# Hybrid attention, retention and MoE layer: attention shares, a stage for retention with three sets of buffers, its decay kept in its units, and no GpSimd in it

## The chip, the cores and the metric

One core of a Trainium2 chip runs the program. The metric is the device time of one execution in microseconds (us), the median over runs. Engine names in the profile: PE is TensorE's matmuls and PEld its weight loads, DVE is VectorE, ACT is ScalarE, POOL is GpSimd, SP is SyncE, which here issues most DMAs.

## The reference

One encoder layer on 2048 tokens of width 1024. A normed input is projected into seven parts, two head groups run beside each other, and a mixture of experts follows.

```python
# attention, 4 heads of 2 maps of 64, values of 128; chunk of 64, causal by chunk
s = einsum(q, k) * scale - slope * |q_pos - k_pos|        # per map
a = softmax(s[0]) - lam * softmax(s[1])
o = rmsnorm(a @ v, subln_g) * (1 - lambda_init)           # lambda_init 0.2
# retention, 4 heads, q and k of 64, v and g of 128, gamma per head
intra = (q @ k.T * 0.125) * decay[t - s >= 0] @ v
cross = (q * gamma**(t + 1)) @ state
state = state * gamma**C + (k * 0.125 * gamma**(C - 1 - s)).T @ v
o = silu(g) * head_rmsnorm(intra + cross)
# then
h = x + concat(att, ret) @ w_out
out = rmsnorm(h + moe(rmsnorm(h)))     # 4 groups top-1, 8 experts each, top-2, SwiGLU
```

## The kernel before

Large products are split in a high and a low part and done as three matmuls (L62, L63, L64 of the helper `mm3`); the result in PSUM is taken out by an ACT copy and a DVE difference (`split_psum`, L54 and L55).

**Projection** (`Proj.run`): 96 units of eight triple matmuls of 512 columns, tile `pa`. Results go to DRAM: QS, KS, VS for the attention, RT (q and k of the retention, transposed), VR and GR (its values and gate).

**Attention** (`att_head`), in three stages of 512-token row groups, (0,1), (2), (3), four heads each. For 128 query rows: scores `pS` (L350, L351) for up to 2048 keys, bias and maximum in one DVE operation (L352), exponent on ACT (L359), the difference of the two maps (reciprocal L362, `c` L363, the long product L366), transposes `pT` (L382), their split (L54, L55), value products `pO`, and in `finish` the norm (a Newton inverse root, L31 to L40, then U times r, L426, and times subg, L427, both on GpSimd).

**Retention** (`retention`), 16 blocks of 128 tokens, two at a time. `prepare` loads one pair ahead: kt, qz (with zeros in the other half), vr, gr; GpSimd forms vd = vr times decay (L481) and qd = qz times decay (L486); the gate is a tanh (L490) and a product (L491). `inner` makes a head pair's q·k (L499), transposes kt (L500), masks with rdec (L502) and copies (L504). Then per head pair: qd·state (L523), A·v (L524), kd·vd (L528), the state's step on DVE (L530). After two blocks come an inverse root (L546, L31 to L40, L548), O times r (L549) and times th (L550) on GpSimd, 1024 elements a partition each, and the store of both blocks. Two sets of the buffers exist (`bufs=2`).

**Out-projection** (`OutProj`): w_out is loaded in eight tiles (L709), split on ACT (L712) and, half of them each, GpSimd and DVE (L713), into woh and wol; the router's weights are cast by DVE (L1129). Then come 16 blocks with 48 matmuls each into `pF`, and the routing. The MoE stage is last.

Order: `merge` emits two streams in turn, by weights: attention beside the projection up to a share FA of all attention, beside retention FR, and the rest beside the out-projection. Pieces of attention are emitted at a higher priority (PRI). A scheduler then fixes each engine's order. SP's loads and stores are one queue in program order.

Of the kernel before, what the change touches and what calls it, by code (L numbers as in the profile page):

```python
# [84 lines left out]
class Proj:  # L85
# [108 lines left out]
    def colT(self, u, c, ct, g):  # L194
# [8 lines left out]
        if c == 3:  # L203
            st = self.stg.tile([128, 512], F32, name="st", tag="st")
            nc.scalar.activation(st, ps, AF.Copy)
            nc.sync.dma_start(k.RT[ct][:, ts], st)
            return
# [9 lines left out]
    def rows(self, u, c, b):  # L217
# [78 lines left out]
def att_head(k, s, h):  # L296
# [119 lines left out]
    def finish(b0, b1):  # L416
# [9 lines left out]
        nc.gpsimd.tensor_mul(u, u, r[:, :, None].to_broadcast([128, n, 128]))  # L426
        nc.gpsimd.tensor_mul(u, u, k.subg[:, None, :].to_broadcast([128, n, 128]))  # L427
# [25 lines left out]
def retention(k):  # L453
    nc, tc = k.nc, k.tc
    V, G = nc.vector, nc.gpsimd
    state, qz = [], {}
    for pr in range(2):
# [3 lines left out]
        for n in range(2):  # L461
# [3 lines left out]
            qz[pr, n] = z  # L465
    def prepare(n):
# [39 lines left out]
    nxt = prepare(0)  # L506
# [3 lines left out]
    for b in range(NB):  # L510
        if b % 2 == 0:
            X = nxt
            nxt = prepare(b // 2 + 1) if b + 2 < NB else None
            vr, O, ss = X.vr, X.O, X.ss
        bb = b % 2
        st2 = []
        for pr in range(2):
            A, kd = st[pr]
            po = k.pF.tile([128, 512], F32, name="pF")
            for s in range(2):  # L520
                ps = po[:, s * 128:(s + 1) * 128]
# [96 lines left out]
def att_consts(k, n):  # L618
# [15 lines left out]
    k.subg = k.bc.tile([128, 128], F32, name="subg")  # L634
    nc.sync.dma_start(k.subg, bcast_rows(k.da_subln_g, 128))
    nc.vector.tensor_scalar(k.subg, k.subg, 0.8, None, op0=OP.mult)


def ret_consts(k):
    nc = k.nc  # L640
    k.rdec = k.br.tile([128, 2, 256], F32, name="rdec", bufs=1)
    k.qdec = k.br.tile([128, 2, 128], F32, name="qdec", bufs=1)
    k.vdec = k.br.tile([128, 4], F32, name="vdec", bufs=1)
    k.sdec = k.br.tile([128, 2], F32, name="sdec", bufs=1)
    rel = k.br.tile([128, 128], F32, name="rel", bufs=1)
# [3 lines left out]
    nc.gpsimd.iota(rel, pattern=[[1, 128]], base=0, channel_multiplier=-1, allow_small_or_imprecise_dtypes=True)
    nc.gpsimd.iota(pos, pattern=[[1, 128]], base=1, channel_multiplier=0, allow_small_or_imprecise_dtypes=True)  # L650
    nc.gpsimd.iota(col, pattern=[[1, 1]], base=127, channel_multiplier=-1, allow_small_or_imprecise_dtypes=True)
    nc.vector.tensor_scalar(msk, rel, 0.0, 0.125, op0=OP.is_ge, op1=OP.mult)
    nc.vector.tensor_scalar(rel, rel, 0.0, None, op0=OP.max)
    for hd in range(4):
        pr, s = hd // 2, hd % 2
        rd = k.rdec[:, pr, s * 128:(s + 1) * 128]
        nc.scalar.activation(rd, rel, AF.Exp, scale=LGAM[hd])
        nc.vector.tensor_mul(rd, rd, msk)
        nc.scalar.activation(k.qdec[s * 64:(s + 1) * 64, pr, :], pos[s * 64:(s + 1) * 64], AF.Exp, scale=LGAM[hd])
        nc.scalar.activation(k.vdec[:, hd:hd + 1], col, AF.Exp, scale=LGAM[hd])  # L660
# [1269 lines left out]
```

## Time and profile before

| | |
|---|---|
| median of 3 runs | 2078.36 us (2072.5 to 2091.58) |
| profiled execution | 2069.81 us |
| its span | 2068.0 us |
| busy PE, DVE, ACT, POOL | 1939.0, 1551.5, 1122.5, 663.0 us |
| granted clock of PE, mean | 0.973 |

The span is counted from the first instruction to the last; the profiled execution's own time is 1.8 us more. Busy time is an average over stages with different limits, so the tables below are by stretch. In the profile, L12 is line 12 of the kernel; what stands behind "<-" in a list of waits is what ended the wait. A matmul's duration in the timeline includes a part that overlaps the next; the distance of two starts is the pace.

### The profile page before, as it was taken

What the parts mean: (1) busy time and instruction counts of PE and PEld (TensorE: products, weight loads), DVE (VectorE), ACT (ScalarE), POOL (GpSimd) and SP (SyncE); (2) the same over time, 40 slices, a digit from 0 to 9 for tenths busy, and PEclk for the clock granted to TensorE, in tenths of its full rate; (3) what the DMA queues carried; (4) which work ended last, traced back from release to release, by engine and by line L of the source; (5) the groups of instructions that cost most, each with busy time, mean ns of one, the idle gap of its engine ahead of it and who ended that gap; (6) DMA issues with size and microseconds to landing.
All of it is one profiled execution on the core that took longest, in us unless ns stands there. A gap on an engine that the chain in (4) does not pass through costs nothing. (4 is left out here: it accounts for less than half of the span.)

```text
span 2068.0 us, 30117 instructions
## 1 busy us (share of the span) xinstructions
PE 1939.0 (94%) x9811; PEld 1539.9 (74%) x9811; DVE 1551.5 (75%) x3462; ACT 1122.5 (54%) x1915; POOL 663.0 (32%) x362
## 2 busy tenths in 40 slices
PE   6999999999999987789999997899999999999994
PEld 5788888788888875578887775677777677777673
DVE  7355446855565578987877767989997899998874
ACT  4244445534444454555454315667776777776763
POOL 0000000010000037421101105777766468755333
PEclk9999999999999999889999997999999999999997
DMA  6655344573675457364453455899999999998993
GB/s 202 199 153 168 117 134 142 183 238 127 204 215 168 138 152 222 128 198 143 148 180 124 139 224 193 288 331 300 318 324 308 325 352 353 349 339 299 332 323 109
DMA packets 241810, 459.61 MB, mean 222 GB/s; under 512 B 27376, under 2 KB 130160, under 8 KB 240624
## 3 DMA queue, kind: packets, MB, share of 16 engines
q1 hardware_dynamic: 224384, 401.53, 57.1%
q0 software_dynamic: 16976, 55.06, 9.9%
q8 instruction: 78, 1.28, 0.2%
q10 hardware_dynamic: 288, 1.05, 0.1%
q14 instruction: 84, 0.69, 0.1%
HBM read 365.81 MB, written 91.75 MB: 221 GB/s over the span
## 5 line engine op out<-in xcount | busy, mean ns | idle before, releaser
L1485 DVE TENSOR_TENSOR ml<-mr,mh 128x1024 fp32r<-128x1024 f32 x376 | 445.6, 1211 | 32.0 <-ACT mh L1484 31.9
L1484 ACT ACTIVATE mh<-mr 128x1024 fp32r<-128x1024 f32 x376 | 385.0, 1054 | 119.1 <-PE acc L74 67.5
L1515 POOL DMA_INDIRECT xg<-XN,TA x120 | 270.0, 2250 | 70.3 <-issue 29.3
L352 DVE CUSTOM_DVE_ANT_0 p<-pS,dist 128x512 f32<-128x512 f32 (+1 forms) x320 | 187.9, 605 | 124.1 <-PE pS L351 116.3
L426 POOL TENSOR_TENSOR U<-U,r 128x512 f32<-128x512 f32 (+2 forms) x13 | 16.5, 1270 | 721.6 <-DVE r L40 619.6
L359 ACT ACTIVATE p<-p,nm 128x128 f32<-128x128 f32 (+15 forms) x128 | 153.9, 1202 | 111.8 <-DVE nm L358 111.6
L64 PE MATMUL acc<-mh,xlo 128*128 128x512 f32 x512 | 204.4, 400 | 1.6 <-DVE xlo L1557 1.6
L63 PE MATMUL acc<-ml,xhi 128*128 128x512 f32 x512 | 204.4, 399 | 0.0
L62 PE MATMUL acc<-mh,xhi 128*128 128x512 f32 x512 | 203.4, 400 | 0.1
L54 ACT ACTIVATE ah<-pT 128x512 fp32r<-128x512 f32 (+2 forms) x176 | 85.4, 498 | 138.8 <-PE pT L382 96.7
L62 PE MATMUL pa<-whi,xh 128*128 128x512 f32 x384 | 151.4, 396 | 3.2 <-ACT whi L161 2.5
L62 PE MATMUL pa<-xh,whi 128*128 128x512 f32 x384 | 152.7, 398 | 1.4 <-DVE st L58 1.4
L63 PE MATMUL pa<-wlo,xh 128*128 128x512 f32 x384 | 152.2, 397 | 1.8 <-DVE wlo L162 1.5
L64 PE MATMUL pa<-whi,xl 128*128 128x512 f32 x384 | 153.0, 399 | 0.0
L63 PE MATMUL pa<-xl,whi 128*128 128x512 f32 x384 | 152.0, 396 | 0.0
L64 PE MATMUL pa<-xh,wlo 128*128 128x512 f32 x384 | 151.6, 395 | 0.0
L162 DVE TENSOR_TENSOR wlo<-wr,whi 128x1024 fp32r<-128x1024 f32 x72 | 90.6, 1260 | 64.3 <-ACT whi L161 62.8
L350 PE MATMUL pS<-kst,qs 128*128 128x512 f32 (+1 forms) x320 | 123.3, 398 | 15.6 <-DVE cm L352 7.3
L55 DVE TENSOR_TENSOR al<-pT,ah 128x512 fp32r<-128x512 f32 (+2 forms) x176 | 97.5, 564 | 44.0 <-ACT ah L54 43.6
L62 PEld LDWEIGHTS acc<-mh,xhi 128*128 128x128 f32 x512 | 97.2, 190 | 32.5 <-ACT y L1646 0.5
L161 ACT ACTIVATE whi<-wr 128x1024 fp32r<-128x1024 f32 x72 | 76.1, 1058 | 78.6 <-PE pa L63 35.9
L64 PEld LDWEIGHTS acc<-mh,xlo 128*128 128x128 f32 x512 | 96.7, 189 | 24.3 <-DVE xlo L1557 2.1
(536 smaller groups left out, 4890.1 us busy)
## 6 DMA issues: line engine op xcount, KB each, us to landing
mr<-in_expert_w_gate_dram SPq DMA_DIRECT2D x128, 512.0 KB, 6.4
mr<-in_expert_w_up_dram SPq DMA_DIRECT2D x128, 512.0 KB, 6.5
mr<-in_expert_w_down_dram SPq DMA_DIRECT2D x128, 512.0 KB, 7.0
wr<-in_w_in_dram SPq DMA_DIRECT2D x72, 512.0 KB, 4.7
vst<-VS SPq DMA_DIRECT2D x72, 256.0 KB, 4.8
qs<-QS SPq DMA_DIRECT2D x128, 128.0 KB, 4.0
st<-in_x_dram SPq DMA_DIRECT2D x16, 512.0 KB, 4.2
VS<-st SPq DMA_DIRECT2D x32, 256.0 KB, 2.9
```

What stands on the lines that cost most here:

```text
L54: nc.scalar.activation(hi, ps, AF.Copy)
L55: return nc.vector.tensor_sub(lo, ps, hi.bitcast(F32))
L62: nc.tensor.matmul(out, s_hi, m_hi, start=start, stop=False)
L63: nc.tensor.matmul(out, s_hi, m_lo, start=False, stop=False)
L64: nc.tensor.matmul(out, s_lo, m_hi, start=False, stop=stop)
L162: nc.vector.tensor_sub(lo, r, hi.bitcast(F32))
L350: nc.tensor.matmul(x, qs[0][:, m, 0, o:o + 128], ks[m][:, a0:a1], start=True, stop=False)
L352: nc.vector.tensor_tensor_reduce(p[:, a0:a1], x, tab[:, c0 + a0:c0 + a1], SLOPES[h], -3.0e38, OP.add, OP.max, accum_out=cm[:, n:n + 1])
L359: nc.scalar.activation(p[:, :nk], p[:, :nk], AF.Exp, bias=nm, accum_out=s0 if m == 0 else s1)
L1484: self.hi_at = nc.scalar.activation(hi, r, AF.Copy)
L1485: self.lo_at = nc.vector.tensor_sub(lo, r, hi.bitcast(F32))
L1515: nc.gpsimd.indirect_dma_start(out=xg[:, g * 256:(g + 1) * 256], out_offset=None, in_=v, in_offset=bass.IndirectOffsetOnAxis(ap=ix[:, g], ...
```

## The change

The key decay is multiplied into k where the projection takes k out of PSUM (DVE, where ACT copied), and silu of the gate is formed there as well. q's decay and the matching inverse drop out: the mask rdec holds a constant per head (gamma^-128, below the diagonal), and the norm's epsilon is scaled per row (edec), since the head norm divides a row's scale out. In `retention`, vd, qd, the tanh and the gate product go, and O's two products become eight DVE operations, one a block and head. Buffers exist in three sets, and `prepare` runs two pairs ahead. In `finish`, U times r runs on DVE, and subg is multiplied into the first four tiles of w_out where they are split; all eight differences run on DVE. Attention gets a share of 0.82 beside the projection; retention is emitted as a stage by itself, after 8 units of attention.

```diff
--- before.py
+++ after.py
@@ Proj.colT
         if c == 3:
             st = self.stg.tile([128, 512], F32, name="st", tag="st")
-            nc.scalar.activation(st, ps, AF.Copy)
+            if ct < 2:
+                nc.scalar.activation(st, ps, AF.Copy)
+            else:
+                nc.vector.tensor_mul(st.rearrange("p (b t) -> p b t", t=128), ps.rearrange("p (b t) -> p b t", t=128),
+                                     k.kdec[:, ct - 2, None, :].to_broadcast([128, 4, 128]))
@@ Proj.rows
-            nc.scalar.activation(st, ps, AF.Copy)
+            if c == 4:
+                nc.scalar.activation(st, ps, AF.Copy)
+            else:
+                nc.scalar.activation(st, ps, AF.Tanh, scale=0.5)
+                nc.vector.scalar_tensor_tensor(st, st, 1.0, ps, op0=OP.add, op1=OP.mult)
@@ att_head, finish
-        nc.gpsimd.tensor_mul(u, u, r[:, :, None].to_broadcast([128, n, 128]))
-        nc.gpsimd.tensor_mul(u, u, k.subg[:, None, :].to_broadcast([128, n, 128]))
+        nc.vector.tensor_mul(u, u, r[:, :, None].to_broadcast([128, n, 128]))
@@ retention
-        for n in range(2):
+        for n in range(3):
             z = k.br.tile([128, 2, 256], F32, name=f"qz{pr}{n}", bufs=1)
...
-        X.q = [qz[pr, n % 2] for pr in range(2)]
+        X.q = [qz[pr, n % 3] for pr in range(2)]
...
-        gr = k.br.tile([128, 2, 512], F32, name="gr")
+        X.th = k.br.tile([128, 2, 512], F32, name="th")
         nc.sync.dma_start(X.vr, k.VR[ts, :].rearrange("(b p) n -> p b n", p=128))
-        nc.sync.dma_start(gr, k.GR[ts, :].rearrange("(b p) n -> p b n", p=128))
-        X.vd = k.br.tile([128, 2, 4, 128], F32, name="vd")
-        G.tensor_mul(X.vd, X.vr.rearrange("p b (h e) -> p b h e", h=4),
-                     k.vdec[:, None, :, None].to_broadcast([128, 2, 4, 128]))
-        X.qd = []
-        for pr in range(2):
-            qd = k.br.tile([128, 2, 2, 128], F32, name=f"qd{pr}")
-            G.tensor_mul(qd, X.q[pr].rearrange("p s (b t) -> p s b t", b=2),
-                         k.qdec[:, pr, None, None, :].to_broadcast([128, 2, 2, 128]))
-            X.qd.append(qd)
-        X.th = k.br.tile([128, 2, 512], F32, name="th")
-        nc.scalar.activation(X.th, gr, AF.Tanh, scale=0.5)
-        V.scalar_tensor_tensor(X.th, X.th, 1.0, gr, op0=OP.add, op1=OP.mult)
+        nc.sync.dma_start(X.th, k.GR[ts, :].rearrange("(b p) n -> p b n", p=128))
...
-    nxt = prepare(0)
+    coming = [prepare(0), prepare(1)]
+    nxt = coming.pop(0)
...
-            nxt = prepare(b // 2 + 1) if b + 2 < NB else None
+            if b + 4 < NB:
+                coming.append(prepare(b // 2 + 2))
+            nxt = coming.pop(0) if coming else None
...
-                    nc.tensor.matmul(ps, X.qd[pr][:, s, bb], state[pr], start=True, stop=False)
+                    nc.tensor.matmul(ps, X.q[pr][:, s, bb * 128:(bb + 1) * 128], state[pr], start=True, stop=False)
...
-            V.tensor_scalar(v, ss.rearrange("p a b -> p (a b)"), 1.0 / 128, EPS, op0=OP.mult, op1=OP.add)
-            rsqrt_newton(nc, rf, v, t_)
-            V.tensor_scalar(rf, rf, 0.5, None, op0=OP.mult)
-            G.tensor_mul(O, O, r[:, :, :, None].to_broadcast([128, 2, 4, 128]))
-            G.tensor_mul(O, O, X.th.rearrange("p a (h e) -> p a h e", h=4))
+            V.scalar_tensor_tensor(v, ss, 1.0 / 128, k.edec[:, None, :].to_broadcast([128, 2, 4]), op0=OP.mult, op1=OP.add)
+            rsqrt_newton(nc, r, v, t_)
+            V.tensor_scalar(r, r, 0.5, None, op0=OP.mult)
+            th = X.th.rearrange("p a (h e) -> p a h e", h=4)
+            for i in range(2):
+                for h in range(4):
+                    V.scalar_tensor_tensor(O[:, i, h], O[:, i, h], r[:, i, h:h + 1], th[:, i, h], op0=OP.mult, op1=OP.mult)
@@ key_decay (new, called ahead of the projection's loop), ret_consts
+def key_decay(k, pool):
...
+        nc.gpsimd.iota(k.kdec[:, pr], pattern=[[-1, 128]], base=127, channel_multiplier=0, allow_small_or_imprecise_dtypes=True)
...
+        nc.scalar.activation(x, x, AF.Exp, scale=LGAM[hd])
+    nc.vector.tensor_scalar(k.kdec, k.kdec, 0.125, None, op0=OP.mult)
...
+        nc.vector.tensor_scalar(k.rdec[:, pr, s * 128:(s + 1) * 128], msk, 0.0, math.exp(-128 * LGAM[hd]), op0=OP.is_ge, op1=OP.mult)
+        nc.scalar.activation(k.edec[:, hd:hd + 1], col, AF.Exp, scale=-2 * LGAM[hd])
...
+    nc.vector.tensor_scalar(k.edec, k.edec, EPS, None, op0=OP.mult)
@@ OutProj.load
-        nc.scalar.activation(hi, r, AF.Copy)
-        (nc.gpsimd if t % 2 < WOP else nc.vector).tensor_sub(lo, r, hi.bitcast(F32))
+        if t < 4:
+            nc.scalar.activation(hi, r, AF.Copy, scale=k.subg)
+            nc.vector.scalar_tensor_tensor(lo, r, k.subg, hi.bitcast(F32), op0=OP.mult, op1=OP.subtract)
+        else:
+            nc.scalar.activation(hi, r, AF.Copy)
+            nc.vector.tensor_sub(lo, r, hi.bitcast(F32))
@@ mixers
-        k.br = ctx.enter_context(tc.tile_pool(name="br", bufs=2, side="right", reuse_waits="tile"))
+        k.br = ctx.enter_context(tc.tile_pool(name="br", bufs=3, side="right", reuse_waits="tile"))
...
-        merge(tc, retention(k), 58, a, na * FR)
+        r = retention(k)
+        next(r)
+        y = 0
+        while y < FR:
+            y += next(a)
+        for _ in r:
+            pass
...
-        merge(tc, op.blocks(at), OB, a, na * (1 - FA - FR))
+        merge(tc, op.blocks(at), OB, a, na * (1 - FA) - FR)
...
-FA = 0.7
-FR = 0.12
+FA = 0.82
+FR = 8.0
```

**PE, end of the projection and start of retention** (pS scores, pO value products and pT transposes of the attention, pa the projection, pF the retention, which begins with L499, L500 of the change). Before:

```order
L63 MATMUL pO<-al,vst 128x256
L64 MATMUL pO<-ah,vst 128x256
L62 MATMUL pO<-ah,vst 128x128
L350 MATMUL pS<-kst,qs 128x512
L351 MATMUL pS<-kst,qs 128x512
L499 MATMUL pF<-qz_8149,kt 128x256
```

and of the change:

```order
L64 MATMUL pa<-whi,xl_4237 128x512
L360 MATMUL pS<-kst,qs 128x512
L361 MATMUL pS<-kst,qs 128x512
L419 MATMUL pT<-ident,oT 128x128 x2
L392 MATMUL pT<-ident,p_6111 128x128 x2
L392 MATMUL pT<-ident,p_6319 128x128 x2
```

About one step of attention moves ahead of the retention's start; in the whole projection it is 5.1 thousand columns of pS, 4.2 of pO and 0.4 of pT more.

**DVE, the last pair of retention's blocks** (r and v the inverse root of the norm, O and th retention's output and gate; p, c, S the attention's). Before:

```order
L40 SCALAR_TENSOR_TENSOR r_9647<-t_9648,r_9647 128x8
L548 TENSOR_SCALAR r_9647<-r_9647 128x8
L362 RECIPROCAL c<-s_7589 128x1
L363 SCALAR_TENSOR_TENSOR c<-c,S_7050,nlam 128x1
L366 SCALAR_TENSOR_TENSOR p_7590<-p_7636,c,p_7590 128x2048
L352 ISA p_7970,cm<-pS,dist 128x512
```

and of the change:

```order
L40 SCALAR_TENSOR_TENSOR r_9747<-t_9748,r_9747 128x8
L551 TENSOR_SCALAR r_9747<-r_9747 128x8
L372 RECIPROCAL c<-s_7210 128x1
L555 SCALAR_TENSOR_TENSOR O<-O,r_9747,th 128x128 x2
L373 SCALAR_TENSOR_TENSOR c<-c,S_6932,nlam 128x1
L555 SCALAR_TENSOR_TENSOR O<-O,r_9747,th 128x128 x6
L376 SCALAR_TENSOR_TENSOR p_7211<-p_7232,c,p_7211 128x2048
L362 ISA p_7544,cm<-pS,dist 128x512
```

The eight products on O stand on DVE between the attention's reciprocal and its long product.

**POOL, in the middle of retention.** Before, a piece of it:

```order
L486 TENSOR_TENSOR qd_9150<-qz_8157,qdec 128x512
L550 TENSOR_TENSOR O<-O,th 128x1024
L481 TENSOR_TENSOR vd<-vr,vdec 128x1024
L486 TENSOR_TENSOR qd_9354<-qz_8152,qdec 128x512
L549 TENSOR_TENSOR O<-O,r_9118 128x1024
L486 TENSOR_TENSOR qd_9356<-qz_8160,qdec 128x512
```

and all that the change leaves on POOL from retention's constants (dist, msk, col) to the first operation of the routing (xc):

```order
L626 IOTA dist 128x1536
L660 IOTA msk 128x128
L661 IOTA col 128x1
L626 IOTA dist 128x2048
L867 TENSOR_TENSOR xc<-xT 128x512 x24
```

No product of retention or of the attention's end is left there.

## Rows read from the trace of the kernel before

**Rows 1.** Stretches: us, busy PE, PEld, DVE, ACT, POOL (instructions), PEclk, DMA share, GB/s

```profile
0.00:733.00 733.00, 711.83 (x3587) 596.26 (x3588) 421.70 (x1192) 328.51 (x654) 30.12 (x58) 1.00 0.55 169
769.50:779.50 10.00, 8.75 (x66) 6.88 (x65) 8.57 (x30) 6.10 (x31) 4.07 (x3) 1.00 0.88 270
779.50:799.30 19.80, 12.46 (x66) 9.60 (x65) 11.62 (x29) 6.15 (x30) 17.34 (x10) 0.74 0.91 279
801.00:845.00 44.00, 37.73 (x242) 28.65 (x241) 43.58 (x124) 26.17 (x90) 26.02 (x13) 1.00 0.46 146
907.00:1240.00 333.00, 323.83 (x2025) 268.57 (x2025) 253.66 (x866) 139.13 (x263) 41.24 (x34) 1.00 0.48 163
```

**Rows 2.** Tile pF: duration ns min/median/max, first and last start, forms

```profile
L62 PE MATMUL pF<-woh,mh x256: 387/393/500, 907.1 to 1239.9; 128*128 128x512 f32 x128
...
L524 PE MATMUL pF<-vr,A x128: 270/275/582, 745.6 to 861.7; 128*128 128x128 f32 x128
...
L499 PE MATMUL pF<-qz,kt x64: 377/379/634, 739.1 to 858.2; 128*128 128x256 f32 x64
```

**Rows 3.** DVE by line and form, 801 to 845: count, busy us, mean ns, idle before

```profile
L352 DVE CUSTOM_DVE_ANT_0 p<-pS,dist 128x512 f32<-128x512 f32 x16 | 10.8, 677 | 0.0
...
L530 DVE SCALAR_TENSOR_TENSOR state<-state,sdec,pF 128x128 f32<-128x128 f32 x12 | 4.0, 336 | 0.0
L491 DVE SCALAR_TENSOR_TENSOR th<-th,gr 128x1024 f32<-128x1024 f32 x3 | 3.6, 1216 | 0.0
L363 DVE SCALAR_TENSOR_TENSOR c<-c,S,nlam 128x1 f32<-128x1 f32 x2 | 3.1, 1548 | 0.0
...
L40 DVE SCALAR_TENSOR_TENSOR r<-t,r 128x8 f32<-128x8 f32 x8 | 2.3, 284 | 0.1
L546 DVE TENSOR_SCALAR v<-ss 128x8 f32<-128x8 f32 x3 | 2.2, 731 | 0.0
...
L39 DVE SCALAR_TENSOR_TENSOR t<-t,v 128x8 f32<-128x8 f32 x8 | 2.1, 260 | 0.1
L31 DVE TENSOR_SCALAR r<-v 128x8 int32<-128x8 int32 x3 | 2.1, 694 | 0.0
```

**Rows 4.** The same view of DVE at the end of the projection, 600 to 733

```profile
L366 DVE SCALAR_TENSOR_TENSOR p<-p,c,p 128x1536 f32<-128x1536 f32 x2 | 3.6, 1819 | 0.1
...
L363 DVE SCALAR_TENSOR_TENSOR c<-c,S,nlam 128x1 f32<-128x1 f32 x8 | 1.8, 219 | 0.3
...
L39 DVE SCALAR_TENSOR_TENSOR t<-t,v 128x4 f32<-128x4 f32 x6 | 1.0, 162 | 0.2
```

**Rows 5.** DVE in order of time, after retention: start us, duration us, instruction

```profile
866.52 2.20 DVE L33 TENSOR_TENSOR t<-r 128x8 f32<-128x8 f32 x1
...
886.38 0.30 DVE L1129 CAST wr<-wor 128x288 bf16<-128x288 f32 x1
...
889.17 4.13 DVE L366 SCALAR_TENSOR_TENSOR p<-p,c,p 128x1664 f32<-128x1664 f32 x1
893.23 2.45 DVE L1129 CAST wr<-wor 128x288 bf16<-128x288 f32 x1
```

**Rows 6.** POOL in order of time, the same stretch

```profile
866.34 2.35 POOL L550 TENSOR_TENSOR O<-O,th 128x1024 f32<-128x1024 f32 x1
870.06 1.90 POOL L549 TENSOR_TENSOR O<-O,r 128x1024 f32<-128x1024 f32 x1 [1.37 <-issue]
872.04 2.34 POOL L550 TENSOR_TENSOR O<-O,th 128x1024 f32<-128x1024 f32 x1
```

**Rows 7.** SP's queue, 730 to 910: waited for, us in total, times, longest

```profile
SPq L709 <- DVE wr L1129: 15.5, 1, 15.5
```

**Rows 8.** PE in order of time: value matmuls of the attention

```profile
886.12 0.28 PE L64 MATMUL pO<-ah,vst 128*128 128x256 f32 x1
886.24 0.28 PE L62 MATMUL pO<-ah,vst 128*128 128x256 f32 x1
```

More of the change, by code (lines that the diff above doesn't have):

```diff
@@ L283, in attention @@
                     yield from att_head(k, s, h)
+            if s + 1 < len(STAGES):
+                k.ready = 4 * STAGES[s + 1][0]
     k.att_done, k.ready = True, NB
@@ L454, in retention @@
     nc, tc = k.nc, k.tc
-    V, G = nc.vector, nc.gpsimd
+    V = nc.vector
     state, qz = [], {}
@@ L527, in retention @@
                 for s in range(2):
-                    nc.tensor.matmul(po[s * 64:(s + 1) * 64, 256:384], kd[:, s * 64:(s + 1) * 64], X.vd[:, bb, 2 * pr + s],
-                                     start=True, stop=True)
+                    nc.tensor.matmul(po[s * 64:(s + 1) * 64, 256:384], kd[:, s * 64:(s + 1) * 64],
+                                     vr[:, bb, (2 * pr + s) * 128:(2 * pr + s + 1) * 128], start=True, stop=True)
                 V.scalar_tensor_tensor(state[pr], state[pr], k.sdec[:, pr:pr + 1], po[:, 256:384], op0=OP.mult, op1=OP.add)
@@ L541, in retention @@
         if bb:
-            v = k.br.tile([128, 8], F32, name="v4")
+            v = k.br.tile([128, 2, 4], F32, name="v4")
             r = k.br.tile([128, 2, 4], F32, name="r4")
-            t_ = k.br.tile([128, 8], F32, name="t4")
-            rf = r.rearrange("p a b -> p (a b)")
-            V.tensor_scalar(v, ss.rearrange("p a b -> p (a b)"), 1.0 / 128, EPS, op0=OP.mult, op1=OP.add)
-            rsqrt_newton(nc, rf, v, t_)
-            V.tensor_scalar(rf, rf, 0.5, None, op0=OP.mult)
-            G.tensor_mul(O, O, r[:, :, :, None].to_broadcast([128, 2, 4, 128]))
-            G.tensor_mul(O, O, X.th.rearrange("p a (h e) -> p a h e", h=4))
+            t_ = k.br.tile([128, 2, 4], F32, name="t4")
+            V.scalar_tensor_tensor(v, ss, 1.0 / 128, k.edec[:, None, :].to_broadcast([128, 2, 4]), op0=OP.mult, op1=OP.add)
[5 more added lines that the diff above has]
+                    V.scalar_tensor_tensor(O[:, i, h], O[:, i, h], r[:, i, h:h + 1], th[:, i, h], op0=OP.mult, op1=OP.mult)
             nc.sync.dma_start(k.MIX[X.rows, 512:1024].rearrange("(b p) n -> p b n", p=128), O.rearrange("p a h e -> p a (h e)"))
@@ L633, in att_consts @@
     nc.vector.scalar_tensor_tensor(k.nlam, ls[:, 1:2], -0.2, ls[:, 0:1], op0=OP.add, op1=OP.subtract)
-    k.subg = k.bc.tile([128, 128], F32, name="subg")
-    nc.sync.dma_start(k.subg, bcast_rows(k.da_subln_g, 128))
-    nc.vector.tensor_scalar(k.subg, k.subg, 0.8, None, op0=OP.mult)
+def key_decay(k, pool):
+    nc = k.nc
+    k.kdec = pool.tile([128, 2, 128], F32, name="kdec", bufs=1)
+    for pr in range(2):
+        nc.gpsimd.iota(k.kdec[:, pr], pattern=[[-1, 128]], base=127, channel_multiplier=0, allow_small_or_imprecise_dtypes=True)
+    for hd in range(4):
+        x = k.kdec[hd % 2 * 64:(hd % 2 + 1) * 64, hd // 2]
+        nc.scalar.activation(x, x, AF.Exp, scale=LGAM[hd])
+    nc.vector.tensor_scalar(k.kdec, k.kdec, 0.125, None, op0=OP.mult)
 def ret_consts(k):
@@ L641, in ret_consts @@
     k.rdec = k.br.tile([128, 2, 256], F32, name="rdec", bufs=1)
-    k.qdec = k.br.tile([128, 2, 128], F32, name="qdec", bufs=1)
-    k.vdec = k.br.tile([128, 4], F32, name="vdec", bufs=1)
+    k.edec = k.br.tile([128, 4], F32, name="edec", bufs=1)
     k.sdec = k.br.tile([128, 2], F32, name="sdec", bufs=1)
-    rel = k.br.tile([128, 128], F32, name="rel", bufs=1)
     msk = k.br.tile([128, 128], F32, name="msk", bufs=1)
-    pos = k.br.tile([128, 128], F32, name="pos", bufs=1)
     col = k.br.tile([128, 1], F32, name="col", bufs=1)
[L649 to L653, printed above, removed]
+    nc.gpsimd.iota(msk, pattern=[[1, 128]], base=0, channel_multiplier=-1, allow_small_or_imprecise_dtypes=True)
+    nc.gpsimd.iota(col, pattern=[[1, 1]], base=1, channel_multiplier=1, allow_small_or_imprecise_dtypes=True)
     for hd in range(4):
         pr, s = hd // 2, hd % 2
[L656 to L660, printed above, removed]
+        nc.vector.tensor_scalar(k.rdec[:, pr, s * 128:(s + 1) * 128], msk, 0.0, math.exp(-128 * LGAM[hd]), op0=OP.is_ge, op1=OP.mult)
+        nc.scalar.activation(k.edec[:, hd:hd + 1], col, AF.Exp, scale=-2 * LGAM[hd])
         nc.vector.memset(k.sdec[s * 64:(s + 1) * 64, pr:pr + 1], math.exp(128 * LGAM[hd]))
-    nc.vector.tensor_scalar(k.vdec, k.vdec, 0.125, None, op0=OP.mult)
+    nc.vector.tensor_scalar(k.edec, k.edec, EPS, None, op0=OP.mult)
 class OutProj:
@@ L680, in __init__ @@
         k.nc.scalar.dma_start(k.ffg, bcast_rows(k.ffn_norm_g, D))
+        k.subg = k.rs.tile([128, 1], F32, name="subg")
+        k.nc.sync.dma_start(k.subg, k.da_subln_g.rearrange("(p o) -> p o", o=1))
+        k.nc.vector.tensor_scalar(k.subg, k.subg, 0.8, None, op0=OP.mult)
         self.W = {}
@@ L886, in mixers @@
     nc, tc = k.nc, k.tc
-    k.att_done, k.ready = False, 4 * STAGES[-1][0]
+    k.att_done, k.ready = False, 0
     na = att_weight()
@@ L890, in mixers @@
         pj = Proj(k, ctx)
+        key_decay(k, pj.sm)
         a = attention(k, pj)
@@ L942 @@
 CUTS = ((13, 12), (16, 14))
-WOP = 1
 PRI = 100
```

## Prediction

> **What bounds the kernel now.** I read the table of busy time by stage first, then the first and last matmuls of the tile pF, then DVE's lines in one saturated stretch against the same lines where GpSimd is quiet, then the rows and waits just ahead of the out-projection. Projection and out-projection are TensorE's: it is busy 711.83 of 733.00 us, and 323.83 of 333.00 [rows 1]. Between them it isn't: retention's matmuls start at 739.1 and end at 861.7, a stage of 122.6 us, and the out-projection's first matmul is at 907.1 [rows 2], 45.4 us later. What fills these two gaps differs by stretch. From 801 to 845 DVE is the limit, busy 43.58 of 44.00 while TensorE has 37.73. From 779.5 to 799.3 no compute engine is full (TensorE 12.46 of 19.80, DVE 11.62), but GpSimd is at 17.34, and the clock is 0.74. These 19.8 us carry 66 matmuls, and so do the 10.00 us ahead of them, where GpSimd is busy 4.07 and the clock is 1.00 [rows 1]: each of the two stretches does two blocks of retention.
>
> DVE's saturation isn't all work. In 801 to 845 the 128x1 product L363 takes 1548 ns and the 128x8 steps L546, L31, L40 and L39 take 731, 694, 284 and 260 [rows 3]; at the end of the projection, with GpSimd idle for most of the time, L363 takes 219 and the same kind of step 162 [rows 4]. In the tail one such step, L33, lasts 2.20 us, from 866.52 to 868.72, and GpSimd's product L550 runs from 866.34 to 868.69 [rows 5, 6]. I read it so: some DVE instructions are held while GpSimd runs.
>
> **The change, part by part.** Sums are against the profiled execution, 2069.81 us; the median of the runs shown is 8.55 above it, and I add that at the end.
>
> *Projection, +4.6.* The orders show how much more attention the larger share buys: over the whole stage 5.1 thousand more columns of scores, 4.2 of value products and 0.4 of transposes, 3% more than before, since attention there runs behind its emission whatever the share. The first fence of the orders shows it: one attention step more. Value matmuls of 256 columns follow each other by 0.12 us [rows 8], so 0.47 us for a thousand columns; TensorE sets the pace there, so 9.7 thousand cost 4.6. The new evictions (16 halves of the gate with a tanh and one DVE product, and decayed keys) run on DVE and ACT, which the stage leaves slack; I price them at nothing. If the cover failed, TensorE would wait for a free accumulator; the nearest row for one of the 16 is a product of 1.22 us [rows 3], so 20 us at most if every one lay bare.
>
> *Out-projection, +3.8.* 8.1 thousand columns more are in it after, by the same count and price; it is TensorE's too.
>
> *Retention, the stretch 779.5 to 799.3: −8.9.* GpSimd's work there (the decay of q and v, both products on O, two on U) is gone, so the two blocks should take the 10.0 us of the bare pair ahead of them plus 0.9 for 2.0 thousand attention columns that still lie there: 19.8 − 10.9. Least gain 0, if the loads set it: the DMA share is 0.91 in one and 0.88 in the other [rows 1], which is why I don't go below the bare pair.
>
> *Retention, 801 to 845: −5.2.* On DVE: held time −7.8 (L363 2 × (1548 − 219) = 2.7; L546 3 × (731 − 162) = 1.7; L31 3 × (694 − 162) = 1.6; L40 and L39 8 each, 1.0 and 0.8); the products on O, eight for two blocks, 24 here, +6.0 at 0.25 us each (from below 1.216/8 = 0.152, L491 with eight times the elements; from above 0.336, L530 of the same shape reading PSUM; so 3.6 to 8.1, and I take the middle); the three gate products L491 −3.6; some 3.2 score chunks fewer by the orders' count at 0.75, −2.4 (0.677 from L352 and its small companion) [rows 3, 4]. That is −7.8, which would leave 36.2 us of DVE. TensorE then has 37.7 less 1.6 for 3.5 thousand columns, 36.1, and two engines don't both run full: at the share TensorE reaches in the bare pair, 8.75 of 10, it would take 41.3, a gain of 2.7. I take the middle of 2.7 and 7.8.
>
> *The rest of the stage: 0.* Its other 58.8 us lose GpSimd's products as well; from nothing to the rate of the saturated stretch, 7.8/44 × 58.8 = −10.4. I take nothing, since loads and the recurrence of the state are seen there too and attention's shift to the last blocks takes some of it back. The second fence of the orders shows what DVE gets in the last pair: eight products more, between the attention's steps. Three sets of buffers let loads go two pairs ahead; on SP's queue they stand ahead of nothing that the out-projection needs.
>
> *The tail, −8.6.* After the last r, GpSimd runs L549 and L550 from 870.06 to 874.38, and SP's w_out loads stand behind that store; the seventh of them waits 15.5 us for the router weights that DVE casts [rows 6, 7]. So the first matmul hangs on this chain: L33 held, 2.20 instead of 0.17, −2.0; 4.3 us of GpSimd become eight DVE products, 2.0, so −2.3; L366 of 1664 takes 4.13 beside GpSimd's L713, where 1819 × 1664/1536 = 1.97 is its own, −2.2; the cast takes 2.45, 0.30 before, −2.1 [rows 4 to 6]. Four more differences L713 move to DVE; they lie in the wait for w_out, else they cost about 4 × 1.22 = 4.9 (by L491's row of as many elements). Bounds 0 and −8.6: I take it whole, since all four lie in one chain.
>
> Sum: +4.6 + 3.8 − 8.9 − 5.2 − 8.6 = **−14.3**: 2055.5 against the profiled execution, 2064 against the median.
>
> **The rivals.**
> 1. *The rest gives too* (0.24): DVE gets all 7.8 in the saturated stretch and the rest of the stage the same rate. −14.3 − 2.6 − 10.4 = −27.3: 2051. For it: the held steps occur wherever GpSimd runs. Against it: the loads.
> 2. *Relief off the path* (0.15): half of the stretch, half of the tail, nothing else. −4.4 − 4.3 + 8.4 = about 0: 2078. For it: the DMA share of 0.91.
> 3. *The clock* (0.04). Most attention in the stage moves to its last three pairs, so four pairs of blocks run nearly bare. In 779.5 to 799.3, where TensorE waited for vr, GpSimd and the state, the clock was 0.74; in the bare pair ahead it was 1.00 [rows 1]. Were all four at the lower level, 1.2 GHz, their 8.75 us of TensorE would double: +35 − 14.3 = +20.7, 2099. The row of the bare pair speaks against it. The Trainium skill, "TensorE: Matmul & The Clock Gate", section "HAM oscillation — how this bites in real kernels", describes just such a pattern, bursts of matmuls with waits between that leave them at half clock; by that rule a stage of bare retention is the worse one, and the 0.74 is in agreement with it, the 1.00 isn't.
> 4. *DVE becomes the bound* (0.09): the held durations aren't GpSimd's doing, so DVE, already at 43.58 of 44, only gets work. 64 products × 0.336 = +21.5, the differences +4.9, eight gate products −9.7, the larger shares +8.4, no other gain: +25, 2103. It decides if L363 still averages over 0.5 us in the stage. Against it: 219 ns where GpSimd rests. The Trainium skill, "Perfetto Trace Analysis", section "Optimizing Scalar/DVE Operations", says that a saturated DVE may gain by giving work to ScalarE or even GpSimd, and that between DVE and GpSimd it may not, as they share a read port; the first half of it is this rival, the second half my forecast.
> That the change doesn't do what it says holds for its first clause, 3% more columns beside the projection, and is in the forecast.
>
> **How the numbers follow.** The forecast, with 2054 to 2072 of its own (the bounds of the saturated stretch and part of the tail), has 0.48. The range is 2042 to 2084: it leaves out rivals 3 and 4 and the outermost parts of 1 and 2, in all 0.18. About 1% (20.8 us) is what a measurement of this kernel can tell from no change, so faster means under 2057.6: nearly all of rival 1 and a fifth of the forecast, 0.33. Slower, over 2099.1: most of rival 4 and half of rival 3, 0.10. The same: 0.57.
>
> **What would show it.** Retention's matmuls, first to last, should span 108 or so, not 122.6, and from the last to the out-projection's first should be some 37, not 45.4. L363 at 0.2 to 0.3 us, the products on O near 0.25, DVE's stalls gone beside a silent GpSimd, the out-projection and projection longer by 4 to 5 each. Wrong it would be if the stage keeps its length with its loads as the releasers, if the O products take over 0.34, if the stage's clock falls under 0.9, or if the first out-projection matmul waits for w_out's own transfer rather than for DVE.

## Result and profile after

The change takes 2069.23 us (median of 20 runs, 2059.73 to 2086.85), the kernel before 2080.07 (20 runs): a ratio of 0.9949, 95% interval 0.9929 to 0.9968, so 11 us less. The forecast was 2064, 14 us less.

One profiled execution is a poor measure of that: the first one of the change took 2086.85 us, a second one 2050.80, and what lies behind the out-projection, which the change leaves alone, took 842 and 811 us in them. The stages ahead of it repeat within 3 us in the change and within 5 before, so both kernels were profiled twice and the stages are compared by their means. Even so a stage's end is known to a few us only: four kernels of the next section (e3, e7, e10, e11) have the change's projection in the same order and end it at 744.9 to 750.9.

| us | before, two profiles | change, two profiles | difference of means | forecast |
|---|---|---|---|---|
| last projection matmul | 732.4, 737.6 | 752.8, 750.0 | +16.4 | +4.6 |
| from it to retention's first | 6.7, 6.7 | 11.9, 12.2 | +5.3 | 0 |
| retention's matmuls | 122.6, 127.5 | 97.8, 96.2 | −28.1 | −14.1 |
| tail to the out-projection's first | 45.4, 45.7 | 33.9, 33.4 | −11.9 | −8.6 |
| out-projection | 333.3, 336.2 | 346.5, 346.4 | +11.7 | +3.8 |
| last out-projection matmul | 1240.4, 1253.7 | 1242.9, 1238.2 | −6.5 | −14.3 |

By stages the gain is 6.5 us, under half of the forecast's 14.3, and most of its terms are off: retention gave twice what I forecast, and the projection and the out-projection took all of that back. The profiled executions themselves differ by 5.3 us in their means, so the table doesn't place the rest of the 11 us.

First the tile pF in the change, as in [rows 2]; L500 and L528 are retention's first and last kind there:

```profile
L62 PE MATMUL pF<-woh,mh x256: 387/393/775, 896.4 to 1242.4; 128*128 128x512 f32 x128
...
L528 PE MATMUL pF<-vr,A x128: 275/275/323, 771.7 to 862.5; 128*128 128x128 f32 x128
...
L500 PE MATMUL pF<-qz,kt x64: 377/379/767, 764.7 to 859.2; 128*128 128x256 f32 x64
```

and the projection's last matmul, before and then in the change:

```profile
L64 PE MATMUL pa<-whi,xl x384: 387/393/775, 14.9 to 732.4; 128*128 128x512 f32 x192
```

```profile
L64 PE MATMUL pa<-whi,xl x384: 387/393/775, 15.7 to 752.8; 128*128 128x512 f32 x192
```

DVE in retention (740 to 870, by line and form, mean ns in the second column behind the bar), the lines that answer to [rows 3]:

```profile
L555 DVE SCALAR_TENSOR_TENSOR O<-O,r,th 128x128 f32<-128x128 f32 x56 | 15.5, 346 | 0.1
...
L39 DVE SCALAR_TENSOR_TENSOR t<-t,v 128x8 f32<-128x8 f32 x24 | 3.9, 164 | 0.4
...
L31 DVE TENSOR_SCALAR r<-v 128x8 int32<-128x8 int32 x8 | 1.3, 168 | 0.1
L549 DVE SCALAR_TENSOR_TENSOR v<-ss,edec 128x8 f32<-128x8 f32 x8 | 1.3, 161 | 0.9 <-ACT junk L537 0.9
...
L373 DVE SCALAR_TENSOR_TENSOR c<-c,S,nlam 128x1 f32<-128x1 f32 x4 | 0.9, 213 | 0.0
```

The steps of 128x8 are back at 161 to 168 ns and L373 at 213: what was 260 to 1548 in [rows 3] was being held. The products on O have a mean of 346, but durations overlap; in order of time eight in a row take 2.19 us, 0.27 each:

```profile
850.90 2.19 DVE L555 SCALAR_TENSOR_TENSOR O<-O,r,th 128x128 f32<-128x128 f32 x8
```

The same stage by stretches (columns as in [rows 1]), its first 17 us and the rest:

```profile
755.00:772.00 17.00, 9.34 (x36) 7.50 (x37) 11.82 (x39) 4.55 (x13) 1.84 (x1) 0.60 0.57 175
772.00:862.00 90.00, 85.11 (x608) 69.76 (x607) 72.64 (x282) 50.24 (x215) 0.00 (x0) 1.00 0.66 209
```

After the start TensorE is busy 85.11 of 90.00 us at a clock of 1.00 and GpSimd does nothing: the stage is now TensorE's, where [rows 1] had DVE in one stretch and no compute engine in another. At the start it isn't: in the handover TensorE mostly waits, the granted clock falls to 0.50, its lower level of 1.2 GHz, and stays there for retention's first 6 us (4 in the second profile):

```profile
768.00:770.00 2.00, 2.00 (x11) 2.00 (x11) 1.11 (x7) 0.76 (x3) 0.00 (x0) 0.50 0.95 271
```

TensorE's waits in the change (us in total, times, longest), 300 to 770, then 865 to 1245, and then 865 to 1245 in the kernel before:

```profile
PE pT L392 <- DVE p L376: 4.2, 1, 4.2
PE pa L62 <- ACT whi L161: 3.1, 1, 3.1
PE pF L500 <- DVE qz L475: 2.6, 1, 2.6
```

```profile
PE pF L745 <- DMA mx<-MIX: 5.7, 2, 5.5
PE pF L62 <- ACT mh L54: 5.7, 6, 1.1
```

```profile
PE pF L733 <- DMA mx<-MIX: 2.8, 1, 2.8
...
PE pF L62 <- ACT mh L54: 0.2, 1, 0.2
```

In the out-projection it is the split mh, on ACT behind other work, six times (0.2 us before), and the attention's last rows by way of mx, 5.7 against 2.8.

### The profile page after: what moved, and what is told of

It is laid out like the page before. It is cut to its first block, busy times and chain, and to the rows that moved or that the text cites. A ratio compares the mean times of both kernels' runs of the same rounds, so it can differ in the third digit from the quotient of the medians.

```text
span 2085.1 us, 30088 instructions
## 1 busy us (share of the span) xinstructions
PE 1948.0 (93%) x9811; PEld 1543.6 (74%) x9811; DVE 1545.3 (74%) x3560; ACT 1110.9 (53%) x1895; POOL 548.8 (26%) x293
## 4 chain that ended last, share of the span: by engine, by line
PE 72%; DMA 9%; issue 6%; DVE 6%; POOL 4%; ACT 3%; SPq 1%; ACTq 0%; DVEq 0%; POOLq 0%
PE pa L62 7%; PE pa L63 7%; PE pa L64 7%; PE acc L64 5%; PE acc L63 5%; PE acc L62 5%; PE acc L72 3%; PE pS L360 3%; PE pF L64 3%; PE pF L62 3%; PE pS L361 3%; PE pF L63 3%; PE acc L74 3%; PE pT L392 2%; DMA fh<-H,perm 2%
## 5 line engine op out<-in xcount | busy, mean ns | idle before, releaser
L369 ACT ACTIVATE p<-p,nm 128x128 f32<-128x128 f32 (+15 forms) x128 | 153.7, 1201 | 99.7 <-DVE nm L368 99.2
L867 POOL TENSOR_TENSOR xc<-xT 128x512 bf16<-128x512 f32 x24 | 30.5, 1272 | 374.4 <-ACT xT L864 366.5
L62 PEld LDWEIGHTS acc<-mh,xhi 128*128 128x128 f32 x512 | 97.3, 190 | 33.4 <-ACT mh L1502 1.1
L63 PEld LDWEIGHTS acc<-ml,xhi 128*128 128x128 f32 x512 | 97.1, 190 | 25.3 <-DVE ml L1503 1.7
```

Source lines behind the costliest of these rows:

```text
L62: nc.tensor.matmul(out, s_hi, m_hi, start=start, stop=False)
L63: nc.tensor.matmul(out, s_hi, m_lo, start=False, stop=False)
L369: nc.scalar.activation(p[:, :nk], p[:, :nk], AF.Exp, bias=nm, accum_out=s0 if m == 0 else s1)
```

## The experiments

Each was timed against the kernel before; the ratio has its 95% interval. Stage lengths are from each run's one profile. Where attention's columns in a stage are named, they are the columns of TensorE's matmuls on pS, pO and pT between the stage's ends, counted in the run's trace; a thousand are 0.47 us at the forecast's price.

| run | ratio to before | projection's end | gap | retention | tail | out-projection |
|---|---|---|---|---|---|---|
| e1 change again | 0.9938 (0.9904 to 0.9971) | 750.0 | 12.2 | 96.2 | 33.4 | 346.4 |
| e2 shares | 0.9979 (0.9940 to 1.0017) | 748.0 | 9.6 | 113.4 | 44.1 | 326.6 |
| e3 junk | 1.0133 (1.0064 to 1.0202) | 744.9 | 12.5 | 136.5 | 49.5 | 326.5 |
| e5 own stage | 1.0102 (1.0047 to 1.0157) | 737.6 | 8.2 | 135.6 | 48.3 | 335.7 |
| e6 plain evictions | 0.9893 (0.9856 to 0.9931) | 740.9 | 7.2 | 99.2 | 40.9 | 343.5 |
| e7 two sets | 0.9945 (0.9909 to 0.9982) | 746.0 | 10.6 | 115.2 | 43.9 | 322.4 |
| e8 handover | 0.9889 (0.9825 to 0.9953) | 739.1 | 8.4 | 96.2 | 32.7 | 347.2 |
| e9 lambda once | 0.9838 (0.9785 to 0.9890) | 738.9 | 8.3 | 105.9 | 37.6 | 335.7 |
| e10 zeros | 0.9913 (0.9880 to 0.9947) | 750.9 | 14.1 | 101.4 | 30.8 | 346.9 |
| e11 O on GpSimd | 0.9922 (0.9887 to 0.9958) | 748.1 | 13.2 | 100.3 | 31.8 | 340.0 |
| e12 handover again | 0.9843 (0.9798 to 0.9887) | 738.4 | 8.4 | 97.8 | 32.6 | 347.5 |

**e1, e4: both kernels once more, unaltered.**

> The changed kernel once more, unaltered, for a second profile of it: in the first one the projection ended 20.4 us later than before (752.8 against 732.4), retention's matmuls spanned 97.8 us (764.7 to 862.5), the out-projection's began 33.9 us after and spanned 346.5 us. If these lengths belong to the kernel, each comes back within 3 us and the MoE stage, 842 us there, falls to some 828 to 835, since that profiled execution took 2086.85 us and the median is 2069. If the projection's extra length is one execution's own, its end comes back at 737 to 742 (my +4.6 us) instead.

> The kernel before once more, unaltered, for a second profile: end of the projection's matmuls (732.4 in the first), retention's 122.6 us, tail 45.4 us, out-projection 333.3 us. If these belong to the kernel they come back within 3 us; if executions differ by more, the two profiles of before and the change can only be compared by their means.

The change's stages came back within 3 us, its rest at 811. Before, the run of 2078.51 us had its stages at the lengths of the table above; it is up to 5 us from the first, more than expected.

**e3: GpSimd's products put back as idle work.**

```diff
 ...
+        for _ in range(2):
+            nc.gpsimd.tensor_mul(gj, X.vr, X.vr)
 ...
+            for _ in range(2):
+                nc.gpsimd.tensor_mul(gj, O.rearrange("p a h e -> p a (h e)"), X.vr)
```

> The changed kernel with four GpSimd products of 128x1024 per pair of blocks added in retention (two on vr at the load, two on the finished O) that nothing reads: 32 in all, at about 1.9 us each some 61 us of GpSimd. Theory (a GpSimd product holds some DVE instructions): retention's 128x1 and 128x8 DVE steps rise from about 0.2 to a mean over 0.5 us, retention's span grows by 8 to 20 us from 98 and the time by as much. Rival (held time is no more than DVE's own queue, or lies off the path): the spans and the time stay within 3 us of the change's.

2098.15 us, 29 more than the change and 37 more than e1; retention 136.5, 39.5 longer than the change's mean of 97.0. Both are over the theory's upper end. DVE by line and form, 740 to 870:

```profile
L39 DVE SCALAR_TENSOR_TENSOR t<-t,v 128x8 f32<-128x8 f32 x16 | 11.6, 725 | 0.2
...
L40 DVE SCALAR_TENSOR_TENSOR r<-t,r 128x8 f32<-128x8 f32 x16 | 8.7, 544 | 0.1
```

then DVE, and GpSimd, in order of time:

```profile
798.65 1.64 DVE L39 SCALAR_TENSOR_TENSOR t<-t,v 128x8 f32<-128x8 f32 x1
...
800.42 1.84 DVE L40 SCALAR_TENSOR_TENSOR r<-t,r 128x8 f32<-128x8 f32 x1
...
802.38 0.34 DVE L537 SCALAR_TENSOR_TENSOR state<-state,sdec,pF 128x128 f32<-128x128 f32 x1
```

```profile
798.37 3.86 POOL L494 TENSOR_TENSOR gj<-vr 128x1024 f32<-128x1024 f32 x2 [11.47 <-DMA vr<-VR]
802.31 4.80 POOL L560 TENSOR_TENSOR gj<-O,vr 128x1024 f32<-128x1024 f32 x2
```

Two GpSimd products share the first POOL row; in the trace the first of them ends at 800.26. L39 began at 798.65, during it, and ended at 800.28. The next step, L40, ends at 802.26, and the second product at 802.23. A small step that starts during a product lasts to its end: in retention and the tail of this run all 20 steps of 128x8 that started more than 0.25 us before a product's end ended 0.02 or 0.03 us after it. The state's step, L537, which reads PSUM, isn't held: begun at 802.38, during the next product (from 802.31), it takes 0.34. But it, and all of retention, stands behind the held steps in DVE's queue. Summed over retention, the held DVE instructions last 35.7 us longer than the same forms do beside an idle GpSimd, an estimate from this trace; the stage is 39.5 longer.

**e5: the emission alone, on the kernel before.**

```diff
 ...
-        merge(tc, retention(k), 58, a, na * FR)
+        r = retention(k)
+        next(r)
+        y = 0
+        while y < FR:
+            y += next(a)
+        for _ in r:
+            pass
 ...
-FA = 0.7
-FR = 0.12
+FA = 0.82
+FR = 8.0
```

> The kernel before with only the change of emission: share 0.82 beside the projection, retention emitted as a stage by itself after 8 units of attention; GpSimd's products, decay, two sets and evictions as before. Its order has the projection's columns of the kernel before, to the last one (so the share does nothing there), and 18 thousand columns of attention less beside the out-projection (141.7 against 165.6). Theory (the gain of retention is GpSimd's silence): retention's span stays at 118 to 130 us, the tail at 44 or more, the projection ends at 732 to 738, and the time is 2075 to 2090. Rival (a stage of its own makes retention short): span under 108 us, time 2060 to 2070.

2098.20 us: slower than expected, retention 135.6. The rival is out: with GpSimd's products in place a stage of its own is the worse order. Its DVE lines, 740 to 870:

```profile
L548 DVE TENSOR_SCALAR v<-ss 128x8 f32<-128x8 f32 x7 | 4.4, 635 | 0.1
L31 DVE TENSOR_SCALAR r<-v 128x8 int32<-128x8 int32 x7 | 4.3, 613 | 0.0
```

**e2: the emission of before, on the change.**

```diff
-        r = retention(k)
 ...
+        merge(tc, retention(k), 58, a, na * FR)
 ...
-FA = 0.82
-FR = 8.0
+FA = 0.7
+FR = 0.12
```

> The changed kernel with the emission of before: share 0.7 of attention beside the projection, 0.12 merged with retention, rest beside the out-projection. Theory (GpSimd's products held DVE, and taking them away is the gain, while the larger shares only move attention): projection ends at 732 to 738 again, retention's span is 105 to 112 us, the tail 34 to 38, the out-projection 333 to 340, and the time is 2060 to 2070, like the change or a little better. Rival (retention got short only because attention left it for the two other stages, and three sets or a silent GpSimd do nothing): retention's span returns to 118 to 125 us and the time to 2078 to 2085.

2071.62 us; retention 113.4, between theory and rival's bounds, the out-projection 20 us shorter, and the last out-projection matmul at 1241.7, where the change has 1242.9 and 1238.2. The emission moves attention between stages and, without GpSimd's products, is worth nothing that these runs can tell. The projection ended at 748.0 though its share was 0.7: the theory's 732 to 738 was wrong, and so the share isn't why it got longer. The tail, 44.1, missed the theory's 34 to 38 as well: 40.6 thousand of attention's columns lie in it, where the change's has 26.8.

**e7: two sets of buffers, one pair ahead.**

```diff
-        for n in range(3):
+        for n in range(2):
 ...
-    coming = [prepare(0), prepare(1)]
+    coming = [prepare(0)]
 ...
-tc.tile_pool(name="br", bufs=3,
+tc.tile_pool(name="br", bufs=2,
```

> The changed kernel with two sets of buffers and one pair prepared ahead, as before. Its order has some 11 thousand attention columns more in the stage (5 us). Theory (GpSimd's silence carries the gain): retention's span is 97 plus 5 to 8, so 102 to 106, and the time within 5 us of the change's. Rival (loads two pairs ahead carry it): span of 112 us or more, with the loads of qz, kt and vr as the releasers of TensorE's waits, and a time of 2075 or more.

2067.92 us, as the theory's time says, but a span of 115.2, as the rival's. Both only in part: attention lies elsewhere again, 62.2 thousand of its columns in retention where the change has 49.9, and the out-projection is 24 us shorter. For the whole the third set is worth nothing that can be told. How much of the span is loads was not separated.

**e11: O's products back on GpSimd.**

```diff
 ...
-                    V.scalar_tensor_tensor(O[:, i, h], O[:, i, h], r[:, i, h:h + 1], th[:, i, h], op0=OP.mult, op1=OP.mult)
+            nc.gpsimd.tensor_mul(O, O, r[:, :, :, None].to_broadcast([128, 2, 4, 128]))
+            nc.gpsimd.tensor_mul(O, O, th)
```

> The changed kernel with only O's two products back on GpSimd as 128x1024 operations (16 in all, about 2 us each, some 34 us of GpSimd); the rest of GpSimd stays silent. Theory (each GpSimd product holds DVE's small steps, and the last pair's two lie on the path to w_out): retention's span grows by 4 to 12 us, the tail by 2 to 5, the time by 5 to 12 to 2072 to 2080. Rival (DVE is saturated, and the eight DVE products for two blocks, 2 us, cost what GpSimd's save): span and time unchanged or 3 to 6 us shorter.

2058.43 us, with an interval that overlaps the change's, and a stage 3 us longer: the theory's time is out, the rival holds, and this piece of the move is neutral. DVE, 740 to 870:

```profile
L549 DVE SCALAR_TENSOR_TENSOR v<-ss,edec 128x8 f32<-128x8 f32 x8 | 3.8, 470 | 0.8 <-ACT junk L537 0.8
...
L373 DVE SCALAR_TENSOR_TENSOR c<-c,S,nlam 128x1 f32<-128x1 f32 x5 | 2.8, 551 | 0.1
```

These two kinds of steps are held (470 and 551 ns), some 4 us, with the attention's held steps some 10 in all, and 64 products of 0.27 us are gone from DVE. A hold costs only where a step that can be held falls into a product; O's products come when r is done, and the next pair's r comes later. So 27.4 us of GpSimd's products cost the stage 3 us here, and 60.4 us cost it 39.5 in e3.

**e6: the plain evictions.**

```diff
 ...
-            if c == 4:
-                nc.scalar.activation(st, ps, AF.Copy)
-            else:
-                nc.scalar.activation(st, ps, AF.Tanh, scale=0.5)
-                nc.vector.scalar_tensor_tensor(st, st, 1.0, ps, op0=OP.add, op1=OP.mult)
+            nc.scalar.activation(st, ps, AF.Copy)
 ...
```

> The changed kernel with the projection's plain evictions of before (ACT copy; the decay of k and the silu of the gate are left out). Theory (the two-step eviction of the gate, ACT then DVE, and the DVE product on k hold up the accumulators, and this is the projection's extra time that I had priced at nothing): the projection ends at 734 to 742 instead of 751, retention's matmuls begin 8 to 15 us earlier, the time is 2055 to 2064. Rival (the extra time is attention's columns, or the loads that stand elsewhere in SP's queue): the projection still ends at 747 or later and the time is within 4 us of the change's.

This kernel leaves out the decay of k and the silu of the gate. 2055.56 us; the projection ends at 740.9, 10 us ahead of the change's mean. By the letter the theory won. But 304.6 thousand of attention's columns lie beside the projection here and 312.3 in the change, which is 3.6 of the 10 us, and in the change's second profile most of TensorE's stalls lie in two stretches, shown below, and what ends them there is not the gate's eviction.

**e8, e9, e10, e12: the handover.** The four lambda rows are loaded, and waited for by DVE, at each of the attention's three stages. SP's queue at the third, in the change's second profile:

```profile
744.13 8.41 SPq L243 DMA_DIRECT2D GR<-st  x2
754.23 0.32 SPq L483 DMA_DIRECT2D kt<-RT  x1
754.64 0.38 SPq L631 DMA_DIRECT2D lam<-in_da_lambda_q_dram  x1
755.07 0.42 SPq L631 DMA_DIRECT2D lam<-in_da_lambda_k_dram  x1
755.55 0.42 SPq L631 DMA_DIRECT2D lam<-in_da_lambda_q_dram  x1
756.02 0.42 SPq L631 DMA_DIRECT2D lam<-in_da_lambda_k_dram  x1
756.50 0.43 SPq L483 DMA_DIRECT2D kt<-RT  x1
757.03 2.53 SPq L487 DMA_DIRECT2D qz<-RT  x4
```

The gate's last store is issued late, since it needs a DVE product; then four lambda loads stand between kt's halves. At the second stage DVE itself waits, with a weight split and an eviction behind it, and TensorE behind these:

```profile
411.64 0.23 DVE L634 TENSOR_TENSOR lam<-lam 128x64 f32<-128x64 f32 x1 [0.65 <-DMA lam<-in_da_lambda_k_dram]
413.76 0.22 DVE L634 TENSOR_TENSOR lam<-lam 128x64 f32<-128x64 f32 x1 [1.90 <-DMA lam<-in_da_lambda_k_dram]
413.91 1.22 DVE L162 TENSOR_TENSOR wlo<-wr,whi 128x1024 fp32r<-128x1024 f32 x1
415.04 0.68 DVE L55 TENSOR_TENSOR st<-pa,st 128x512 fp32r<-128x512 f32 x1
```

```profile
415.78 0.51 PE L62 MATMUL pa<-xh,whi 128*128 128x512 f32 x1 [0.74 <-DVE st L55]
```

```diff
 ...
-            V.memset(z[0:64, 1], 0.0)
-            V.memset(z[64:128, 0], 0.0)
+            nc.gpsimd.memset(z[0:64, 1], 0.0)
+            nc.gpsimd.memset(z[64:128, 0], 0.0)
 ...
+    if hasattr(k, "nlam"):
+        return
-    lam = k.bc.tile([128, 4, 64], F32, name="lam")
+    lam = k.nl.tile([128, 4, 64], F32, name="lam")
 ...
```

> The changed kernel with a shorter handover from projection to retention: the zeros of qz are set by GpSimd, idle there, instead of by DVE between the attention's steps, and the four lambda rows are loaded once instead of at each of the attention's three stages, so no lambda load stands between kt's halves. Theory (the 12 us from the projection's last matmul to retention's first, 6.7 before, are DVE's memsets and those loads): the gap falls to 6 to 9 us and the time by 3 to 6, to about 2063. Rival (the gap is the last store of the gate and the attention's long product): it stays at 11 to 13 us and the time is the change's.

> The changed kernel with one half of the shorter handover: the lambda rows are loaded once, at the attention's first stage; DVE still sets the zeros of qz. In the change DVE stands 2.5 us for those rows at 411 to 414 us with a weight split and an eviction behind it in its queue. Theory (the lambda rows stall DVE in the middle of the projection and kt's second half at the handover): the projection's stalls between 400 and 450 us go, it ends at 738 to 743, and 8 to 14 of the 15 us that both halves gave come back: 2053 to 2061. Rival (the zeros of qz on DVE were it): the projection ends at 748 or later and the time stays at 2063 to 2070.

> The other half: the zeros of qz by GpSimd, the lambda rows loaded three times as in the change. Theory: the projection ends at 748 to 753 as in the change, the gap to retention's first matmul falls from 12 to 9 or 10 us, and the time is 2060 to 2067. Rival (the zeros were the cause): the projection ends under 743.

> Both halves of the shorter handover again, in more rounds, beside their parts: if it is better than the change, 2048 to 2056 us, a ratio of 0.986 to 0.990 to the kernel before, and stage lengths within 3 us of the first profile (projection's end 739.1, retention 96.2, tail 32.7, out-projection 347.2). If the first measurement was a lucky one, 2060 to 2066.

Both halves: 2051.31 and 2049.95 us; 3 to 6 us were expected of them, and 18 came, most of it ahead of retention. The lambda half alone: 2049.11. The zeros alone: 2064.38, projection's end 750.9; the gap, which was to fall to 9 or 10 us, is 14.1. So it is the edit of the lambda rows: the three kernels with it end the projection at 738.4 to 739.1, the six with the change's projection at 744.9 to 752.8, 10 us later in the mean. Stretches of 50 us (columns as in [rows 1]), in the change's second profile and with one load, and the projection's last matmul with one load:

```profile
400.00:450.00 50.00, 44.77 (x225) 36.27 (x224) 31.59 (x76) 20.64 (x42) 1.43 (x1) 1.00 0.78 237
550.00:600.00 50.00, 45.80 (x221) 38.00 (x220) 32.71 (x76) 22.42 (x40) 0.00 (x0) 0.97 0.70 219
```

```profile
400.00:450.00 50.00, 48.48 (x244) 39.38 (x243) 32.05 (x72) 21.01 (x42) 1.41 (x1) 1.00 0.80 240
550.00:600.00 50.00, 49.94 (x248) 41.61 (x247) 34.11 (x77) 25.57 (x44) 0.00 (x0) 1.00 0.86 263
```

```profile
L64 PE MATMUL pa<-whi,xl x384: 387/393/776, 15.9 to 738.9; 128*128 128x512 f32 x192
```

TensorE loses 5.2 and 4.2 us in two stretches of the change, 1.5 and 0.1 with one load. The second loss, in the change's second profile, is one wait for a weight load, which SP issued behind loads of vst and qs:

```profile
554.92 1.05 SPq L147 DMA_DIRECT2D wr<-in_w_in_dram  x2
```

```profile
563.58 0.73 PE L62 MATMUL pa<-whi,xh 128*128 128x512 f32 x2 [4.20 <-ACT whi L161]
```

In e6 the rows are loaded three times too, but the order puts DVE's reading later and it doesn't wait:

```profile
413.79 0.22 DVE L626 TENSOR_TENSOR lam<-lam 128x64 f32<-128x64 f32 x1
...
414.53 0.22 DVE L626 TENSOR_TENSOR lam<-lam 128x64 f32<-128x64 f32 x1
```

The evictions cost little by themselves: e9 keeps them and ends the projection at 738.9, 3.9 us behind the mean of the kernel before (735.0), and the 8.7 thousand more of attention's columns in it (311.3 against 302.6) are 4.1 us. What the edit of the rows gains is traced only in part. DVE's wait for the rows holds TensorE directly for the 0.74 us above; with one load SP issues the weight loads at 546.30 and 551.32, ahead of those of qs; and e6, with three loads of the rows, loses at most 0.2 us in the two stretches. So most of the gain isn't that wait but the order that came with the edit, as far as it is traced, and whether another new order would give it with three loads was not tried. e9 and e12 are the best versions here: 2049.11 and 2049.95 us, their intervals (up to 0.9890) below the change's (from 0.9929).

## Why the prediction came out as it did

*Projection, +4.6: measured +16.4.* The step that failed is "The new evictions … run on DVE and ACT, which the stage leaves slack; I price them at nothing". I asked for the evictions' cover and not what moves when the order is made anew: e9 gives 10 to 12 us back with those evictions in place, e6 10 without them, 3.6 of which are columns. Why the change's order stalls where e9's doesn't stays open. The columns were counted and priced rightly and explained wrongly: in e5's order the larger share moves no column beside the projection.

*The handover, forecast 0: measured +5.3.* I wrote that the loads "stand ahead of nothing that the out-projection needs" and didn't ask what stands ahead of them. e9 has 8.3 us there, e1 12.2.

*Retention, −14.1: measured −28.1.* The mechanism is shown by e3 (idle GpSimd work takes all of it back, and the held steps add up to it) and by e5 (the order alone doesn't give it). It isn't the whole: attention has 55.0 thousand columns in the stage before and 49.9 in the change. With GpSimd as silent, e9 has 55.8 and spans 105.9, e2 60.4 and 113.4, e7 62.2 and 115.2. So some 19 us come with about as much attention as before, and the other 9 go along with less of it; where it stays, in e2 and e7, the out-projection is 20 and 24 us shorter. The size failed at "The rest of the stage: 0" and at the middle taken for the saturated stretch; rival 1's −8.9 − 7.8 − 10.4 = −27.1 meets what the stage did in number, though a part of that is attention's. The middle of 0.25 for a product was near (0.27).

*The tail, −8.6: measured −11.9.* In the change none of the four steps is held, and SP's loads of w_out wait at most 4.7 us, for the differences of its tiles, where they waited 15.5 for the cast [rows 7]:

```profile
SPq L717 <- DVE wol L722: 7.9, 2, 4.7
```

But the chain isn't shown to give it all: e2 and e7, with GpSimd as silent, have tails of 44.1 and 43.9, with 40.6 and 41.3 thousand of attention's columns in them, where the kernel before has 32.5 and the change 26.8. How much of the −11.9 is the chain and how much attention that lies elsewhere stays open. The products on O stand between the last r and w_out's loads, on GpSimd in e11 and on DVE in the change, and make no difference there (31.8, and 33.9 and 33.4), so that one link of the chain, −2.3, isn't borne out.

*Out-projection, +3.8: measured +11.7.* The columns by count, and two waits, mh and mx, of 5.5 and 2.9 more, that I did not look for, since I priced it by columns alone.

*Rivals.* The clock's didn't come: after its first 6 us retention's pairs ran at 1.00, where the stretch with GpSimd had 0.74 [rows 1]; the lower level shows in the handover, where TensorE waits, and in those 6 us. DVE didn't become the bound: it is busy 72.64 of 90.00 us. Rival 1's length came for the stage, and losses outside it brought the sum back: by stages the gains are 17 us over the forecast (retention, tail) and the losses 25 (projection, handover, out-projection). That the time lies in the range is luck: terms that were wrong cancel.

## What to carry to other kernels

A change that reorders everything is to be read by stage, with two profiles of each kernel, and each term checked even when the sum fits; count what moved between the stages before a stage's gain is put down to one cause. Loading four small rows of constants once instead of three times gave 10 us of the projection here, though the wait for them held TensorE for under 1: an edit that small can be worth its run. GpSimd's work was worth moving where small DVE steps of a recurrence fell into it, and not where it came after them (e11).

## Not expected of the hardware

A DVE step of 128x8 that starts during a GpSimd product of 128x1024 ends with that product, to 0.03 us (e3: 800.28 and 800.26, 802.26 and 802.23), and a step of 128x128 that reads PSUM keeps its 0.34 us there, while 16 such products placed after r cost the stage 3 us (e11).
